# Group norm and store of an SSD chunk, issued inside the next chunk

## The chip, the cores and the metric

The kernel runs on one core of a Trainium2 chip. Five engines work from queues of their own, each in the order in which its instructions stand: PE (TensorE, matrix products; PEld is its weight load), DVE (VectorE), ACT (ScalarE), POOL (GpSimd) and SP (SyncE, which here only issues transfers). They wait for each other by semaphores. The metric is the time of one execution on the device in microseconds, the median of three.

## The reference

One step of a decoder layer over 1040 prompt rows (16 of them learned) and 32 sample rows (8 sequences of 4), with D = 1024, float32:

```
u    = rmsnorm(h);  proj = u @ w_in          # columns: conformer 2048 | z 1024 | x/B/C 1536 | dt 16
c    = silu(layernorm(dwconv31(glu(conf))))  # group A, 1024 channels
y    = ssd(silu(dwconv4(xbc)), dt)           # group B, 16 heads of 64, 2 groups, state 128, chunks of 128
y    = group_rmsnorm(y * silu(z))            # mean of squares over each group's 512 channels
h    = h + concat(c, y) @ w_out
h    = h + ffn(rmsnorm(h))                   # w_up, dwconv3, silu gate, w_down
out  = rmsnorm(h)                            # and the states of all convolutions and of the scan
```

The change concerns the line with `group_rmsnorm`. In the SSD each chunk needs the state that the chunk before it left; the norm of a chunk is needed by nothing in the scan, only by the product with `w_out`.

## The kernel before

Channels lie on partitions, rows (time) on the free axis. Products are done with each operand split into a high and a low part and three matmuls (L215 to L217, PE stage name `mm`), and the weights of a 128-column tile come by one transfer (`wr`), which ACT casts to the high part `wh` (L204) and DVE subtracts to the low part `wl` (L205).

The order of the program's middle is a list of items, `ORDER` (L59). `p` is a block of 128 conformer channels: its products, and then its convolution of width 31 on DVE, 44 multiply-adds of 128x520 in three running sums `fp` (L535), `fo` (L538) and `fs` (L541), each begun by ACT (L532, L533, L539) and joined by L544 to L547, which write the block's plane of the tile `gq`. `x` and `z` are tiles of the input projection (z tiles are evacuated by ACT at L589 and go through SiLU). `s0` and `s1` are the next SSD chunk of group 0 and 1, `q0` and `q1` the sample rows, `r0` and `r1` the sample states. `l` is a block of rows of the layer norm: it transposes all eight planes of `gq` (L862, `pt`), takes statistics on DVE (L863, L866), normalizes (`cn`, L874 on DVE, L876 on ACT) and transposes back (L883, `pb`). `h` splits the result, `c` are tiles of the product of group A with `w_out`, `y` loads and splits the normed `y` of group B.

A chunk (`ssd`, L667) loads `xc`, transposes it (L679), transposes B and forms B·C in one PSUM tile `pbt` (L696, L697), which ACT (`bt`, L698) and DVE (`cbm`, L700) evacuate. Decay matrices `ab` follow (ACT L724, L725; DVE L726), then the products `pd` (L731), `po` (L713) and the state `pst` (L751); `et` collects y on DVE (L739 to L745), is gated by z (L769) and squared by ACT (L770). The norm is L771 to L782: two sums over planes on DVE (L773, L774, `zs`), a matmul with ones that leaves the mean square of each row (L775, `pn`), DVE adds epsilon (L156), POOL raises to the power -1/2 (L157), ACT puts the result on a diagonal (L779, `rs`), a second matmul spreads it over partitions (L780, `pn` again), DVE multiplies (L781) and SP stores to `y_d` (L782). `pbt` and `pn` share a PSUM pool of two buffers (`small`), `cbm` and `zs` share a tag of two buffers; tiles of one tag are given out in the order in which the code asks for them.

No engine's queue is written by hand here. A scheduler goes through all instructions when the program is built and places, engine by engine, that ready one whose priority number is lowest. The number is the place in the code; evacuations and weight splits are raised to the front (`prio(URGENT)`), and the width-31 convolution is put behind everything else (`prio(CVP)`, CVP = 1,000,000, L523). So what is late in the code fills gaps, and the convolution fills what is left. At run time nothing is rearranged.

Of the kernel before, what the change touches and what calls it, by code (L numbers as in the profile page):

```python
# [7 lines left out]
F = mybir.dt.float32  # L8
R = mybir.dt.float32r
AF = mybir.ActivationFunctionType  # L10
ALU = mybir.AluOpType
# [3 lines left out]
P = 128  # L15
# [47 lines left out]
def hybrid_kernel(ctx: ExitStack, tc: tile.TileContext, a: dict, outs: list):  # L63
    nc = tc.nc
# [3 lines left out]
    @contextmanager  # L68
    def prio(p):
        old = tc.cur_priority  # L70
        tc.cur_priority = p
        yield
        tc.cur_priority = old
# [16 lines left out]
    y_d = dram.tile([D, T], F, name="y_d")  # L90
# [4 lines left out]
    def fmv(d):  # L95
        return d.rearrange("(k p) t -> p k t", p=P)
# [7 lines left out]
    def bank(nm):  # L104
        return ps_bk.tile([P, 512], F, tag="bk", name=nm)
# [4 lines left out]
    def small(nm):  # L110
        return ps_sm.tile([P, 512], F, tag="sm", name=nm)
# [12 lines left out]
    ident = const.tile([P, P], F, name="ident")  # L124
# [7 lines left out]
    ones = const.tile([P, P], F, name="ones")  # L132
# [3 lines left out]
    ones_g = const.tile([P, 1], F, name="ones_g")  # L136
# [17 lines left out]
    def rsqrt(dst, src, n, w=1):  # L154

        nc.vector.tensor_scalar(dst, src, EPS, None, op0=ALU.add)  # L156
        nc.gpsimd.tensor_tensor(dst, dst, mhalf[:n].to_broadcast([n, w]), op=ALU.pow)  # L157
# [68 lines left out]
    def gemm(w, kk, mh, ml, evac, chunks=(0, 1, 2), ch=CH, **kw):  # L226
        for ci in chunks:
            evac(ci, *ch[ci], products(w, kk, mh, ml, ci, ch=ch, **kw))
# [41 lines left out]
    with ExitStack() as s0:  # L270
# [28 lines left out]
        rt = [p0.tile([P, 3], F, name=f"rt{g}") for g in range(3)]  # L299
# [284 lines left out]
    def emit_z(j):  # L584
        zt = px_.tile([P, 1096], F, tag="xo", name="zo", bufs=XO)[:, 0:T]

        def ev(ci, c0, n, ps):
            with prio(URGENT):
                nc.scalar.copy(zt[:, c0:c0 + n], ps[:, :n])  # L589

        in_tile(2 * D + j * P, ev)
        nc.scalar.activation(zt, zt, AF.Silu)
        nc.sync.dma_start(z_d[j * P:(j + 1) * P, :], zt)
# [69 lines left out]
    hT = [None, None]  # L663
    sp = [None]
    left = {}

    def ssd(g, c, t0, L, mask, first=False, sample=False):  # L667
        p2 = sp[0]
        hna, xda, xdt_, xde_, rld = ((HNA0, XDA0, XDT0, XDE0, RLD0), (HNA1, XDA1, XDT1, XDE1, RLD1))[g]
        cols = slice(t0, t0 + L)  # L670
# [27 lines left out]
        nc.scalar.copy(bt[:L], pb[:L, 0:P])  # L698
        cbm = p2.tile([P, P], F, tag="cbm", name="cbm", bufs=2)
        nc.vector.tensor_tensor(cbm[:L, :L], pb[:L, P:P + L], mask[:L, :L], op=ALU.mult)  # L700
        et = p2.tile([P, 4, P], F, tag="et", name="et", bufs=2)
        if not first:
            for s in range(2):
# [45 lines left out]
        if not sample:  # L749
# [5 lines left out]
            else:  # L755
# [4 lines left out]
                else:  # L760
                    nc.vector.tensor_tensor(h8(hn), h8(hT[g]), cdt[:, c, hg:hg + 8].unsqueeze(2).to_broadcast([P, 8, 64]),
                                        op=ALU.mult)
# [3 lines left out]
        zt = p2.tile([P, 4, P], F, tag="zt", name="zt", bufs=2)  # L766
        nc.sync.dma_start(zt[:, :, :L], fmv(z_d)[:, 4 * g:4 * g + 4, cols])
        y = et[:, :, :L]
        nc.vector.tensor_tensor(y, y, zt[:, :, :L], op=ALU.mult)  # L769
        nc.scalar.activation(zt[:, :, :L], y, AF.Square)  # L770
        pn = small("pn")  # L771
        zs = p2.tile([P, P], F, tag="cbm", name="zs", bufs=2)
        nc.vector.tensor_tensor(zt[:, 0:2, :L], zt[:, 0:2, :L], zt[:, 2:4, :L], op=ALU.add)  # L773
        nc.vector.tensor_tensor(zs[:, :L], zt[:, 0, :L], zt[:, 1, :L], op=ALU.add)  # L774
        nc.tensor.matmul(pn[:L, 0:1], zs[:, :L], ones_g, start=True, stop=True)  # L775
        rt = p2.tile([P, 1], F, tag="rt", name="rt")
        rsqrt(rt[:L], pn[:L, 0:1], L)
        rs = p2.tile([P, P], F, tag="rs", name="rs", bufs=2)
        nc.scalar.activation(rs[:L, :L], ident[:L, :L], AF.Copy, scale=rt[:L])  # L779
        nc.tensor.matmul(pn[:, P:P + L], ones[:L, :], rs[:L, :L], start=True, stop=True)  # L780
        nc.vector.tensor_tensor(y, y, pn[:, P:P + L].unsqueeze(1).to_broadcast([P, 4, L]), op=ALU.mult)  # L781
        nc.sync.dma_start(fmv(y_d)[:, 4 * g:4 * g + 4, cols], y)  # L782

    def sample_h0(g, b, place):
        pool, tag = place
# [49 lines left out]
                nc.sync.dma_start(o_sssm[0, b, 8 * g:8 * g + 8].rearrange("(q two) p n -> (two p) q n", two=2), h0)  # L835

    def ssd_state_out(g):
        ph = bank("ph")
        for q in range(4):
            nc.tensor.transpose(ph[:, q * P:(q + 1) * P], hT[g][:, q * P:(q + 1) * P], ident)  # L840
        hs = sp[0].tile([P, 4, P], F, tag="zt", name="hs", bufs=2)
        nc.scalar.copy(hs.rearrange("p q n -> p (q n)"), ph)
        nc.sync.dma_start(o_pssm[0, 0, 8 * g:8 * g + 8].rearrange("(q two) p n -> (two p) q n", two=2), hs)

    def ssd_group(g):
        for c in range(8):
            yield lambda c=c: ssd(g, c, 128 * c, 128, tri, first=(c == 0))
        yield lambda: ssd(g, 8, 1024, 16, tri)
        yield lambda: ssd_state_out(g)
# [37 lines left out]
    def split_c():  # L887

        c_hi.extend(quad(f"c_hi{i}", R) for i in range(2))
        c_lo.extend(quad(f"c_lo{i}", R) for i in range(2))  # L890
        for c0, n in CHO:
            for i in range(2):
                c, hi = gq[i][:, :, c0:c0 + n], c_hi[i][:, :, c0:c0 + n]
                nc.scalar.copy(hi, c)
                nc.vector.tensor_tensor(c_lo[i][:, :, c0:c0 + n], c, hi.bitcast(F), op=ALU.subtract)
# [23 lines left out]
    def load_hr(p, m):  # L919
        c0, n = HALF[p]  # L920
        nc.sync.dma_start(H[p][:, m, 0:2 * n], ob_d[m * P:(m + 1) * P, c0:c0 + 2 * n])

    def out_c(m):
        hr = row_tile("hr")
        rows = slice(m * P, (m + 1) * P)
        nc.sync.dma_start(hr[:, F0:T], h_d[rows, F0:T])

        def ev(ci, c0, n, ps):
            with prio(URGENT):
                nc.vector.tensor_tensor(hr[:, c0:c0 + n], ps[:, :n], hr[:, c0:c0 + n], op=ALU.add)  # L930
            if ci == 2:
                nc.sync.dma_start(ob_d[rows, F0:T], hr[:, F0:T])

        return load_w(w_out[0:D, rows], KD), ev
# [40 lines left out]
    for it, item in enumerate(items):  # L975
        kind = item[0]
        if kind == "p":
            emit_pair(int(item[1:]))
        elif kind == "x":
            emit_xbc(int(item[1:]))  # L980
        elif kind == "z":
            emit_z(int(item[1:]))
        elif kind == "d":
            with tc.using_default_side("right"), tc.tile_pool(name="pdt", bufs=1) as sp[0], prio(URGENT + 3):
                emit_dt()
            with tc.using_default_side("right"):
                sp[0] = sd.enter_context(tc.tile_pool(name="ssd", bufs=1))
            work = {0: list(ssd_group(0)), 1: list(ssd_group(1))}
        elif kind == "s":
            work[int(item[1:])].pop(0)()  # L990
        elif kind == "q":
            ssd(int(item[1:]), 9, NP, NS, btri, sample=True)
        elif kind == "r":
            sample_states(int(item[1:]))
        elif kind == "l":
            if len(lblocks) == 5:
                sc.close()
                lnp = lns.enter_context(tc.tile_pool(name="pln", bufs=1))
            with prio(LNP if LNP is not None else tc.cur_priority):
                ln_part(lnp, gq, *lblocks.pop(0))  # L1000
            if not lblocks:
                lns.close()
                pfv = ctx.enter_context(tc.tile_pool(name="pfv", bufs=1))
                ffnv = pfv.tile([P, 44, 20], F, name="ffnv")
                pq = fs_.enter_context(tc.tile_pool(name="pq", bufs=1))
                ph0 = hs.enter_context(tc.tile_pool(name="ph0", bufs=6))
        elif kind == "h":
            split_c()
        elif item == "c0":

            first2 = [out_c(m) for m in range(2)]
            for ci in range(3):
                for w, ev in first2:
                    gemm(w, KD, qk(c_hi), qk(c_lo), ev, (ci,), CHO)
        elif kind == "c":
            if item == "c7":
                for m in range(KD - 1):
                    load_hr(0, m)
            w, ev = out_c(int(item[1:]))
            gemm(w, KD, qk(c_hi), qk(c_lo), ev, ch=CHO)  # L1020
        elif kind == "y":
            g = int(item[1:])
            if first_y is None:
                first_y = g
                y_quads(0, qb)
                hs.close()
                open_out()
            split_y(0, g, lambda: tmp_tile("yt"))
        if it == last_ssd:
            assert not work[0] and not work[1]  # L1030
            sd.close()
    load_hr(0, KD - 1)
    sx.close()
# [356 lines left out]
    for i in range(2, KF):  # L1390
        w = pair_weights(i)
        for p in range(2):
# [4 lines left out]
            if (i, p) == (KF - 1, 1):  # L1397
                g = g_tiles(0)
# [110 lines left out]
    for c in range(3):  # L1509
        if c == 2:  # L1510
            last_norm = LastNorm()
        hc, g = down(c, g, after)
# [32 lines left out]
```

## Time and profile before

| | |
|---|---|
| median of three runs | 1611.01 us (1605.16 to 1611.17) |
| profiled execution, its own time | 1602.27 us |
| its span, first to last instruction | 1600.6 us |
| PE busy | 1536.9 us, 96% of the span |
| DVE, ACT, POOL busy | 1164.3, 895.7, 40.4 us |
| mean granted TensorE clock | 0.980 of full speed |

The span is the time from the first to the last instruction of the profiled execution; 1.7 us lie around it. Busy PE is not PE at its peak, since the ends of matmuls are modelled; the three 358-column matmuls of a split product start some 0.16 us apart where nothing holds them. The SSD chunks lie between 334 and 732 us of the span, and the layer norm's first blocks between 534 and 565 us. The granted clock has two levels, 1.0 (2.4 GHz) and 0.5 (1.2 GHz).

### The profile page before, as it was taken

Reading aid. Unit: us, or ns where it says so; the run is one execution under the profiler, and the core shown is the slowest. Engines: PE = TensorE matmul, PEld = TensorE weight load, DVE = VectorE, ACT = ScalarE, POOL = GpSimd, SP = SyncE. Lnnn points to the kernel's source line nnn. Section 1 sums busy time; section 2 is a strip of 40 time slices with the busy share of each in tenths; the row PEclk is TensorE's granted clock in tenths of the full one; section 3 lists DMA queues with packets and bytes.
Section 4 is the critical chain, followed back from the end, with each engine's and each line's share of the span. In section 5 each row is a group of like instructions: output and inputs, shape, how many; then the busy total and the mean of one; then the engine's idle time right before and its main releaser. Section 6 shows DMA issues by size and latency. Waiting matters only on the chain.

```text
span 1600.6 us, 28038 instructions
## 1 busy us (share of the span) xinstructions
PE 1536.9 (96%) x10716; PEld 1479.4 (92%) x10716; DVE 1164.3 (73%) x1881; ACT 895.7 (56%) x2160; POOL 40.4 (3%) x99
## 2 busy tenths in 40 slices
PE   6899999999999799998999999999999999999997
PEld 5899999997999688887999999999999998999997
DVE  4799989996897758465668787777777776464343
ACT  6635545478968576684335556656655665353232
POOL 2000000000000000000000000000000000000000
PEclk9999999999999899999989999999999999999998
DMA  6321312166435329667753222222222228766553
GB/s 245 112 69 58 99 45 72 57 179 160 111 115 155 101 70 268 184 172 237 241 171 107 90 84 90 81 73 70 76 83 80 83 79 273 231 204 198 154 161 108
DMA packets 306229, 209.90 MB, mean 131 GB/s; under 512 B 28453, under 2 KB 285017, under 8 KB 306079
## 3 DMA queue, kind: packets, MB, share of 16 engines
q1 hardware_dynamic: 302654, 198.26, 41.8%
q0 software_dynamic: 1056, 5.24, 0.9%
q10 hardware_dynamic: 2384, 4.60, 0.8%
q8 instruction: 84, 1.38, 0.4%
q14 instruction: 51, 0.41, 0.1%
HBM read 157.69 MB, written 51.22 MB: 131 GB/s over the span
## 4 chain that ended last, share of the span: by engine, by line
PE 81%; DMA 6%; issue 5%; DVE 4%; ACT 2%; POOL 1%; SPq 1%; POOLq 0%; DVEq 0%; ACTq 0%
PE mm L216 11%; PE mm L215 11%; PE mm L217 11%; PE X L1249 5%; PE X L1250 5%; PE X L1251 5%; PE mmd L1429 3%; PE mmd L1427 3%; PE mmd L1428 3%; PE Z L1251 2%; PE Z L1250 2%; PE Z L1249 2%; PE Y L1250 1%; PE Y L1249 1%; PE Y L1251 1%
## 5 line engine op out<-in xcount | busy, mean ns | idle before, releaser
L204 ACT CAST wh<-wr 128x768 fp32r<-128x768 f32 (+1 forms) x130 | 131.1, 1009 | 253.6 <-PE mm L216 107.1
L215 PE MATMUL mm<-u_hi,wh 128*128 128x358 f32 (+1 forms) x816 | 268.8, 329 | 0.9 <-ACT sg L245 0.9
L217 PE MATMUL mm<-u_hi,wl 128*128 128x358 f32 (+1 forms) x816 | 268.3, 329 | 0.0
L216 PE MATMUL mm<-u_lo,wh 128*128 128x358 f32 (+1 forms) x816 | 267.6, 328 | 0.0
L205 DVE TENSOR_TENSOR wl<-wr,wh 128x768 fp32r<-128x768 f32 (+1 forms) x130 | 152.4, 1173 | 109.5 <-ACT wh L204 105.2
L1250 PE MATMUL X<-tq,wh 128*128 128x264 f32 (+1 forms) x640 | 183.4, 287 | 0.0
L1249 PE MATMUL X<-tq,wh 128*128 128x264 f32 (+1 forms) x640 | 183.0, 286 | 0.0
L1251 PE MATMUL X<-tq,wl 128*128 128x264 f32 (+1 forms) x640 | 182.7, 285 | 0.0
L1429 PE MATMUL mmd<-g,wl 128*128 128x352 f32 x528 | 171.4, 325 | 1.8 <-DVE wl L205 1.8
L1427 PE MATMUL mmd<-g,wh 128*128 128x352 f32 x528 | 171.5, 325 | 0.9 <-ACT wh L204 0.9
L1428 PE MATMUL mmd<-g,wh 128*128 128x352 f32 x528 | 169.8, 322 | 0.0
L215 PEld LDWEIGHTS mm<-u_hi,wh 128*128 128x128 f32 x816 | 153.6, 188 | 1.6 <-ACT sg L245 1.1
L217 PEld LDWEIGHTS mm<-u_hi,wl 128*128 128x128 f32 x816 | 154.0, 189 | 0.6 <-issue 0.3
L216 PEld LDWEIGHTS mm<-u_lo,wh 128*128 128x128 f32 x816 | 153.5, 188 | 0.5 <-issue 0.4
L1250 PEld LDWEIGHTS X<-tq,wh 128*128 128x128 f32 x640 | 121.7, 190 | 0.0
L1249 PEld LDWEIGHTS X<-tq,wh 128*128 128x128 f32 x640 | 120.9, 189 | 0.3 <-ACT arena L1267 0.3
L1251 PEld LDWEIGHTS X<-tq,wl 128*128 128x128 f32 x640 | 121.0, 189 | 0.0
L1342 DVE SCALAR_TENSOR_TENSOR cv<-arena,ffnv,cv 128x528 f32<-128x528 f32 (+1 forms) x88 | 67.8, 771 | 65.7 <-ACT cv L1339 65.7
L1429 PEld LDWEIGHTS mmd<-g,wl 128*128 128x128 f32 x528 | 99.3, 188 | 3.4 <-DVE wl L205 3.3
L1267 ACT COPY arena<-X 128x266 f32<-128x266 f32 (+2 forms) x200 | 63.2, 337 | 69.4 <-PE X L1251 66.7
L1427 PEld LDWEIGHTS mmd<-g,wh 128*128 128x128 f32 x528 | 99.2, 188 | 1.5 <-ACT wh L204 1.1
L1428 PEld LDWEIGHTS mmd<-g,wh 128*128 128x128 f32 x528 | 99.7, 189 | 0.0
(337 smaller groups left out, 3885.8 us busy)
## 6 DMA issues: line engine op xcount, KB each, us to landing
wr<-in_w_down_dram SPq DMA_DIRECT2D x48, 512.0 KB
wr<-in_w_in_dram SPq DMA_DIRECT2D x36, 512.0 KB
wr<-in_w_out_dram SPq DMA_DIRECT2D x24, 512.0 KB
wr<-in_w_up_dram SPq DMA_DIRECT2D x24, 512.0 KB
spare<-in_w_up_dram SPq DMA_DIRECT2D x20, 512.0 KB
wr<-in_w_down_dram SPq DMA_DIRECT2D x24, 384.0 KB
ab<-acs_d SPq DMA_DIRECT2D x32, 256.0 KB
h<-in_state_ssm_dram SPq DMA_DIRECT2D x32, 256.0 KB
```

Source lines behind the costliest of these rows:

```text
L204: nc.scalar.copy(hi[:, :kk, :], raw[:, :kk, :])
L205: nc.vector.tensor_tensor(lo[:, :kk, :], raw[:, :kk, :], hi[:, :kk, :].bitcast(F), op=ALU.subtract)
L215: mm = [nc.tensor.matmul(ps[:, :n], hi[:, k, :], xh, start=(j == 0), stop=False), nc.tensor.matmul(ps[:, :n], hi[:, k, :], xl, start=False ...
L216: nc.tensor.matmul(ps[:, :n], hi[:, k, :], xl, start=False, stop=False),
L217: nc.tensor.matmul(ps[:, :n], lo[:, k, :], xh, start=False, stop=(j == kk - 1))]
L1249: tick([nc.tensor.matmul(ps[:, :n], hi[:, k, :], bh[:, k, :], start=start and k == 0, stop=False, **kw), nc.tensor.matmul(ps[:, :n], hi[:, ...
L1250: nc.tensor.matmul(ps[:, :n], hi[:, k, :], bl[:, k, :], start=False, stop=False, **kw),
L1251: nc.tensor.matmul(ps[:, :n], lo[:, k, :], bh[:, k, :], start=False, stop=(k == 3), **kw)])
L1342: nc.vector.scalar_tensor_tensor(co[:, j0:nj], fb[:, k + j0:k + nj], ffnv[:, m, 16 + k:17 + k], co[:, j0:nj], op0=ALU.mult, op1=ALU.add)
L1427: nc.tensor.matmul(ps[:, :n], hi[:, k, :], xh, start=(k0 + k == 0), stop=False)
L1428: nc.tensor.matmul(ps[:, :n], hi[:, k, :], xl, start=False, stop=False)
L1429: nc.tensor.matmul(ps[:, :n], lo[:, k, :], xh, start=False, stop=(k0 + k == KF - 1))
```

## The change

The norm becomes a function `norm` that `ssd` puts on a list instead of running it. The next call of `ssd` (the sample rows' too) takes it off and runs it behind its own `pbt` transposes and `cbm`; `ssd_state_out`, the last item of a group, runs what is left. Nothing is computed in another way, and every engine issues the same number of instructions. What changes is each norm's place in the code, so its priority number, and the order in which `pbt`, `pn`, `cbm` and `zs` are asked for. The norm of the eighth chunk of group 0 now belongs to the first `s1`, which stands behind four z tiles, the five items `l` and `h`.

```diff
+    norms = []
...
         nc.vector.tensor_tensor(cbm[:L, :L], pb[:L, P:P + L], mask[:L, :L], op=ALU.mult)
+        if norms:
+            norms.pop(0)()
         et = p2.tile([P, 4, P], F, tag="et", name="et", bufs=2)
...
         nc.scalar.activation(zt[:, :, :L], y, AF.Square)
-        pn = small("pn")
-        zs = p2.tile([P, P], F, tag="cbm", name="zs", bufs=2)
...
-        nc.sync.dma_start(fmv(y_d)[:, 4 * g:4 * g + 4, cols], y)
+
+        def norm():
+            pn = small("pn")
+            zs = p2.tile([P, P], F, tag="cbm", name="zs", bufs=2)
+            nc.vector.tensor_tensor(zt[:, 0:2, :L], zt[:, 0:2, :L], zt[:, 2:4, :L], op=ALU.add)
+            nc.vector.tensor_tensor(zs[:, :L], zt[:, 0, :L], zt[:, 1, :L], op=ALU.add)
+            nc.tensor.matmul(pn[:L, 0:1], zs[:, :L], ones_g, start=True, stop=True)
+            rt = p2.tile([P, 1], F, tag="rt", name="rt")
+            rsqrt(rt[:L], pn[:L, 0:1], L)
+            rs = p2.tile([P, P], F, tag="rs", name="rs", bufs=2)
+            nc.scalar.activation(rs[:L, :L], ident[:L, :L], AF.Copy, scale=rt[:L])
+            nc.tensor.matmul(pn[:, P:P + L], ones[:L, :], rs[:L, :L], start=True, stop=True)
+            nc.vector.tensor_tensor(y, y, pn[:, P:P + L].unsqueeze(1).to_broadcast([P, 4, L]), op=ALU.mult)
+            nc.sync.dma_start(fmv(y_d)[:, 4 * g:4 * g + 4, cols], y)
+
+        norms.append(norm)
...
     def ssd_state_out(g):
+        while norms:
+            norms.pop(0)()
```

In the changed kernel the lines of `ssd` stand 2 to 6 lines further down (`pbt` L698 and L699, `cbm` L702, `ab` L730, `zs` L780, the two `pn` matmuls L781 and L786, the product with `pn` L787), later ones 10 lines (layer norm: `pt` L872, statistics L873 and L876, `pb` L893). All queues are word for word the same up to the first chunk's second half and again from the product with `w_out` of group B on. Between them they differ in many places; three matter below, all where the layer norm begins.

ACT, before, where it begins the convolution of the eighth and last conformer block (`fp` L532; `h0T` are states of the sample rows of `q0`, `hT` is the scan's state of group 0):

```order
L694 ACTIVATE xde<-ptx,dss 128x64 x8
L698 COPY bt<-pbt 128x128
L744 ACTIVATE xc<-xc,dbc 128x128 x3
L579 ACTIVATE xo<-xo 128x1040
L580 ACTIVATE fb<-xo 128x32
L532 ACTIVATE fp<-gq_130,confv 128x521
L533 ACTIVATE fo<-gq_130,confv 128x520
L744 ACTIVATE xc<-xc,dbc 128x32 x3
L801 COPY h0T<-ph 128x512
```

and the same start in the changed kernel:

```order
L589 COPY zo<-mm 128x358
L728 ACTIVATE ab<-ab,acs 128x128 x3
L729 ACTIVATE ab<-ab 128x512
L823 CAST rr<-kept 32x128
L532 ACTIVATE fp<-gq_130,confv 128x521
L204 CAST wh<-wr 128x1024
L589 COPY zo<-mm 128x356
L533 ACTIVATE fo<-gq_130,confv 128x520
```

The start has moved from ahead of the sample rows of `q0` to behind them and behind the next chunk of group 0 and the decays `ab` of the first chunks of group 1, into the third of the last four z tiles.

DVE, before, where that convolution ends and the layer norm's statistics (`BN_STATS`, tile `bs`) begin:

```order
L541 SCALAR_TENSOR_TENSOR fs<-fz,fsum,fs 128x520 x8
L545 TENSOR_TENSOR fs<-fs,fp 128x520
L546 TENSOR_TENSOR gq_130<-fs,fo 128x520
L863 BN_STATS bs<-pt 128x6 x3
L866 BN_AGGR mv<-bs 128x2
L205 TENSOR_TENSOR wl<-wr,wh 128x1024
L156 TENSOR_SCALAR mv<-mv 128x1
L700 TENSOR_TENSOR cbm<-pbt,tri 128x128
L868 SCALAR_TENSOR_TENSOR mv<-mv 128x1
L726 TENSOR_TENSOR ab<-ab,cbm 128x512
L874 TENSOR_SCALAR cn<-pt,mv 128x512
```

and in the changed kernel from the same `wl` on:

```order
L205 TENSOR_TENSOR wl<-wr,wh 128x1024
L702 TENSOR_TENSOR cbm<-pbt,tri 128x128
L780 TENSOR_TENSOR zs<-zt 128x128
L730 TENSOR_TENSOR ab<-ab,cbm 128x512
L156 TENSOR_SCALAR rt<-pn 128x1
...
L535 SCALAR_TENSOR_TENSOR fp<-gq_130,confv,fp 128x521
L787 TENSOR_TENSOR et<-et,pn 128x512
...
L538 SCALAR_TENSOR_TENSOR fo<-gq_130,confv,fo 128x520
...
L544 TENSOR_TENSOR gq_130<-fp,fo 128x520
...
L541 SCALAR_TENSOR_TENSOR fs<-fz,fsum,fs 128x520 x10
L545 TENSOR_TENSOR fs<-fs,fp 128x520
L546 TENSOR_TENSOR gq_130<-fs,fo 128x520
```

The last piece leaves rows out. In full, 25 of the 44 multiply-adds stand behind the `wl`, 24 of them behind the product with `pn` at L787 (3 on `fp`, 6 on `fo`, 15 on `fs`); before, all 44 stood ahead of the `wl`.

PE, before, from the last products of the z tiles to the layer norm's first transposes back:

```order
L862 MATMUL pt<-ident,gq_130 128x128 x2
L215 MATMUL mm<-u_hi_126,wh 128x356
L216 MATMUL mm<-u_lo_128,wh 128x356
L217 MATMUL mm<-u_hi_126,wl 128x356
L696 MATMUL pbt<-ident,xc 128x128
L697 MATMUL pbt<-xc 128x128
L883 MATMUL pb<-ident,cn 128x128 x14
```

and now:

```order
L217 MATMUL mm<-u_hi_126,wl 128x356
L698 MATMUL pbt<-ident,xc 128x128
L699 MATMUL pbt<-xc 128x128
L781 MATMUL pn<-ones_g,zs 128x1
L698 MATMUL pbt<-ident,xc 128x128
L699 MATMUL pbt<-xc 128x128
L786 MATMUL pn<-rs,ones 128x128
L872 MATMUL pt<-ident,gq_130 128x128 x2
L893 MATMUL pb<-ident,cn 128x128 x12
```

The two transposes of the eighth block's plane (`pt<-ident,gq_130 x2`), which need L546, stood six products ahead of the end of the z tiles; they now stand behind it, behind the norm of group 0's eighth chunk, with no product between that norm and them.

## Rows read from the trace of the kernel before

**Rows 1.** PE's waits by who was waited for, 340 to 535 us.
```profile
PE pn L775 <- DVE zs L774: 3.0, 4, 1.0
PE pn L780 <- ACT rs L779: 2.9, 7, 0.6
```
**Rows 2.** The same, 565 to 735 us (total us, times, longest).
```profile
PE pn L780 <- ACT rs L779: 4.0, 7, 2.0
```
**Rows 3.** The same, 735 to 760 us.
```profile
PE mm L215 <- ACT y_hi L910: 2.0, 3, 1.2
PE mm L216 <- DVE y_lo L911: 1.4, 3, 0.8
```
**Rows 4.** One norm in order of time: start, us, engine, line.
```profile
390.78 0.29 DVE L774 TENSOR_TENSOR zs<-zt 128x128 f32<-128x128 f32 x1
...
391.22 0.35 PE L775 MATMUL pn<-ones_g,zs 128*128 128x1 f32 x2 [1.04 <-DVE zs L774]
...
391.68 0.16 DVE L156 TENSOR_SCALAR rt<-pn 128x1 f32<-128x1 f32 x1 [0.61 <-PE pn L775]
...
392.29 0.33 PE L215 MATMUL mm<-u_hi,wh 128*128 128x356 f32 x1
...
393.01 0.49 PE L780 MATMUL pn<-rs,ones 128*128 128x128 f32 x2 [0.40 <-ACT rs L779]
...
393.26 0.41 PE L216 MATMUL mm<-u_lo,wh 128*128 128x356 f32 x1
```
**Rows 5.** PE in order of time where the layer norm begins.
```profile
534.98 0.32 PE L217 MATMUL mm<-u_hi,wl 128*128 128x356 f32 x1
535.14 0.27 PE L696 MATMUL pbt<-ident,xc 128*128 128x128 f32 x1
535.25 0.39 PE L697 MATMUL pbt<-xc 128*128 128x128 f32 x2
540.07 3.94 PE L883 MATMUL pb<-ident,cn 128*128 128x128 f32 x14 [4.44 <-DVE mv L868]
```
**Rows 6.** DVE in order of time, last block's convolution and first layer-norm block.
```profile
517.24 0.76 DVE L538 SCALAR_TENSOR_TENSOR fo<-gq,confv,fo 128x520 f32<-128x520 f32 x1
517.91 0.75 DVE L541 SCALAR_TENSOR_TENSOR fs<-fz,fsum,fs 128x520 f32<-128x520 f32 x1
...
526.04 6.31 DVE L541 SCALAR_TENSOR_TENSOR fs<-fz,fsum,fs 128x520 f32<-128x520 f32 x8
532.39 0.70 DVE L545 TENSOR_TENSOR fs<-fs,fp 128x520 f32<-128x520 f32 x1
533.12 0.70 DVE L546 TENSOR_TENSOR gq<-fs,fo 128x520 f32<-128x520 f32 x1
...
536.41 1.21 DVE L205 TENSOR_TENSOR wl<-wr,wh 128x1024 fp32r<-128x1024 f32 x1
537.53 0.15 DVE L156 TENSOR_SCALAR mv<-mv 128x1 f32<-128x1 f32 x1
...
538.52 0.68 DVE L726 TENSOR_TENSOR ab<-ab,cbm 128x512 f32<-128x512 f32 x1
539.12 0.80 DVE L874 TENSOR_SCALAR cn<-pt,mv 128x512 f32<-128x512 f32 x1
```
**Rows 7.** ACT in order of time: start of that convolution, and end of the z tiles.
```profile
472.69 0.82 ACT L532 ACTIVATE fp<-gq,confv 128x521 f32<-128x521 f32 x1 [0.62 <-DVE fs L545]
...
535.18 1.04 ACT L204 CAST wh<-wr 128x1024 fp32r<-128x1024 f32 x1 [3.61 <-PE mm L216]
...
536.48 0.27 ACT L698 COPY bt<-pbt 128x128 f32<-128x128 f32 x1
```
**Rows 8.** Busy us (x count) of PE, PEld, DVE, ACT, POOL; PEclk, DMA share, GB/s.
```profile
535.00:565.00 30.00, 20.66 (x100) 16.54 (x100) 19.06 (x41) 17.48 (x28) 3.62 (x6) 0.72 0.24 72
537.80:544.60 6.80, 4.40 (x18) 3.14 (x19) 3.08 (x8) 4.57 (x9) 1.46 (x2) 0.50 0.92 256
745.00:750.00 5.00, 4.23 (x19) 3.66 (x18) 2.24 (x4) 2.21 (x3) 0.00 (x0) 0.66 0.84 262
```

More of the change, by code (lines that the diff above doesn't have):

```diff
@@ L770, in ssd @@
         nc.scalar.activation(zt[:, :, :L], y, AF.Square)
-        pn = small("pn")
-        zs = p2.tile([P, P], F, tag="cbm", name="zs", bufs=2)
[L773 to L781, printed above, removed]
-        nc.sync.dma_start(fmv(y_d)[:, 4 * g:4 * g + 4, cols], y)
+        def norm():
[12 more added lines that the diff above has]
+        norms.append(norm)
     def sample_h0(g, b, place):
@@ L1029, in hybrid_kernel @@
         if it == last_ssd:
-            assert not work[0] and not work[1]
+            assert not work[0] and not work[1] and not norms
             sd.close()
```

## The prediction

> **What bounds the kernel now.** I read the page's table of busy time first, then PE's waits stretch by stretch, and last the order of time where a wait is long. PE bounds the kernel: nearly everything is a stream of products, and a microsecond in which PE stands is a microsecond of the total. So the reader should look for PE's waits between 334 and 760 us, since the queues are the same outside.
>
> In the scan the waits are small and of one kind. From 340 to 535 us PE waits 3.0 us for `zs` ahead of the norm's first matmul and 2.9 us for `rs` ahead of its second [rows 1]; from 565 to 735 us 4.0 us more for `rs`, 2.0 of them in one place [rows 2]. One norm in order of time shows why [rows 4]: from the first matmul at 391.22 us over DVE, POOL and ACT to the second at 393.01 us take 1.79 us, and the queue holds only two small transposes and four products between them; the last product starts at 392.29 us, so its successor could have come at about 392.45, and the norm's second matmul is some 0.5 us too early in the queue. Behind it stand products that need nothing from the norm; they start only afterwards (393.26 us). PE does not overtake.
>
> The Trainium skill says the same ("TensorE: Matmul & The Clock Gate", The mechanism): matmuls start and end in strict program order. By that rule nothing fills a gap at run time, and the rows of this norm agree; if PE could pull products forward, neither today's waits nor the hole that I forecast below would cost anything and the change would be worth about nothing.
>
> The largest single wait is elsewhere: where the layer norm begins PE has run out of products at 535.6 us and stands 4.44 us for DVE's `mv` [rows 5]. DVE had finished the last convolution at 533.82 us, its last three rows ending in L546 [rows 6], so before the change convolution and z products end together.
>
> **The change part by part.** No instruction is added or taken away, stores and loads included: 20 norms with their 20 stores move. So there are only waits to count, in three places. I count them from the profiled execution, 1602.27 us, which is 8.74 us under the median of 1611.01.
>
> *The layer norm's start.* ACT began the eighth block's convolution at 472.69 us [rows 7]. In the changed queue that start stands in the third of the last four z tiles, behind the first of its evacuations in the piece of ACT above: in products, 96 ahead of the end of the z tiles, 96 x 0.16 = 15.4 us plus some 2 us of transposes, so at about 518 us or later. And 25 of the 44 multiply-adds stand behind the `wl` that needs the weight buffer which the last z product frees. That anchor is firm: the last z product starts at 534.98 us [rows 5], ACT casts `wh` at 535.18 for 1.04 us [rows 7], so `wl` can run from 536.3 to 537.4 (1.12 us to its successor at 537.53 [rows 6]). From there on DVE, in order:
>
> - `cbm` (0.1) and `zs`, with `bt` on ACT long done (536.48 + 0.27 [rows 7]): about 537.6; from `zs` to the first norm matmul 0.44 and on to `rt` 0.46 [rows 4]: 538.5;
> - `ab`, `cbm` and one multiply-add run in the shadow of the chain over POOL and ACT, 391.68 to 393.01 = 1.33 us, then the second matmul and DVE's product with it, about 0.5 to its start and 0.6 for it, and one `ab` (0.6; each by its spacing in [rows 6]): 541.5;
> - 24 multiply-adds. Where sums alternate they start 0.67 us apart (517.24 and 517.91), where one sum runs alone 0.79 (6.35 us for 8, 526.04 to 532.39) [rows 6]. 14 x 0.67 + 10 x 0.79 = 17.3 us: 558.8;
> - L544, L547 (0.6 + 0.15, estimated as tiles of the same and of a smaller size), L545 0.73, L546 0.70 [rows 6]: 561.0.
>
> Before, the same point was 533.82. PE has only the two transposes ahead of `pb` to do once the norm is through at about 540.0: it stands from there. From L546 to `pb` took 540.07 - 533.82 = 6.25 us; of the DVE work in it `wl` (1.12), two `ab` (about 0.6 each, up to 539.12 [rows 6]) and `cbm` (0.1) are gone, 2.4 us, of which I count 2.2. `pb` at 561.0 + 4.05 = 565.1 instead of 540.07: **25.0 us later**. The cover that kept this hidden, products on PE while DVE convolves, is used up at 535.3 us, since the next products need the layer norm itself.
>
> Bounds: if ACT's start came so late that DVE is not through its first 19 multiply-adds at 536.3, it is more. 518 + about 3 us for ACT's queue + 19 x 0.67 + one `wl` (1.1) = 535; so at most 2 us more. If the DVE chain from `wl` on hides its first 4 us altogether, 21.
>
> *The waits in the norms.* Counting PE's queue between a norm's two matmuls by these spacings (0.16 a product, 0.5 a set of four small ones, 1.05 a state product), before 14 of 20 norms have 0.9 to 1.4 us of work there, against the 1.7 to 1.8 that the chain takes. In the changed queue the first matmul stands further behind `zs`, and 8 norms are short, by 0.1 to 0.45 us: 2.7 us against 8.5 before by the same count. So of the 5.9 us ahead of the layer norm [rows 1] I take 3.5 as saved (0 to 5.9: `zs` may come late again), of the 4.0 behind it [rows 2] 2.5 (0 to 4.0; a wait of ACT like that of 2.0 us may return anywhere).
>
> *The hand-over to the product of group B.* The last norm ends 38 queue rows ahead of the first product with `y_hi` before, 66 rows after: 28 x 0.16 = 4.5 us more for the last store, the load and the split. PE waited 2.0 + 1.4 us for that [rows 3], and the granted clock was 0.66 over 745 to 750 us [rows 8], 5 x 0.34 = 1.7 us. Of these 5.1 us I take 3.5 (0 to 5.1).
>
> Weight and state transfers keep their places against the products that need them; the stores that SP now issues later block nothing that PE waits for, apart from a load or two of `ab` and `xc`, which I take at nothing (0 to 2 us).
>
> **Sum:** +25.0 - 3.5 - 2.5 - 3.5 = +15.5 us. 1602.27 + 15.5 = 1617.8 in the profile's terms, and 1611.0 + 15.5 = 1626.5 against the median: I predict **1626 us**.
>
> **The rivals.**
>
> *The waits go and no hole opens* (faster). Were DVE to finish the convolution at about 534 us as before, what is left is -3.5 - 2.5 - 3.5 = -9.5, at the ends -15: 1601 us. For it speaks that the norm's waits are what the trace shows most often in the scan [rows 1, 2]; the Trainium skill's advice ("Perfetto Trace Analysis", Optimization Strategy) is to find the gaps on the engine that matters and make what they wait for start sooner, and by that advice alone one expects this. It decides at ACT's L532: it would have to run some 25 us sooner than its queue allows, and DVE's L546 stands behind PE's `pn` in any case. 4 in 100.
>
> *The hole is largely paid back* (no change). The layer norm's stage already stands or crawls: clock 0.72 over 535 to 565 us, PE busy 20.66 of 30 [rows 8]. With the chunks of group 1 further ahead in their `cbm` and `ab`, this stage and the scan behind it could give back their 9 us of standing and the waits all their 15: 25 - 17 to 25 - 24, about +4: 1615 us. Against it: the layer norm's own chain is not shortened beyond the 2.2 us counted. 10 in 100.
>
> *The hole and a colder layer norm* (slower still). PE was granted half clock from 537.8 to 544.6 [rows 8] after standing 4.44 us. After standing over 20 us the whole stage to 565 may run at that level; 0.72 against 0.50 over the 20.7 busy us is 20.7 x 0.22 / 0.5 = 9 us at most, and with none of the savings: 1611 + 25 + 5 = 1641 us. 8 in 100.
>
> **How the numbers follow.** My forecast has 78 in 100. A change within 0.5%, 8 us, is about what three runs of this kernel can't tell from none (its own spread is 6 us). The forecast's own bounds are +25.0 - 15.0 = +10 to +27; less the run spread at the low end and towards the colder stage at the high end the range is 1612 to 1639. Slower by over 0.5% (over 1619): nearly all of the forecast and all of the colder case, 0.85; same 0.11; faster 0.04.
>
> **What would show it.** PE in order of time near 540 us: one gap of 20 to 25 us ahead of the layer norm's transposes, ended by DVE's L546, with DVE busy with L535, L538 and L541 all through it. L532 on ACT near 518 to 522 us instead of 472.69. Fewer waits `pn <- rs`, together under 4 us outside the hole. `y_hi` waits under 1 us. The prediction is wrong if that gap is under 10 us (the convolution came sooner), or if the gap is there and the time is not, because the stages behind it ran shorter by more than 15 us.

## The result and the profile after

The changed kernel takes 1632.82 us in the median of four runs (1631.89 to 1636.49), the kernel before 1608.94 us beside it; the ratio is 1.016 (95% interval 1.0138 to 1.0182), so 23.9 us slower. The forecast was 1626 us in a range of 1612 to 1639. The profiled execution after took 1633.08 us (span 1631.4), near its median; that of before took 1602.27 us (span 1600.6), 6.7 us under the median of 1608.94.

PE in order of time where the layer norm begins, the answer to [rows 5] (start, us, engine, line; in brackets the wait and who ended it):

```profile
534.64 0.33 PE L217 MATMUL mm<-u_hi,wl 128*128 128x356 f32 x1
...
537.92 0.38 PE L781 MATMUL pn<-ones_g,zs 128*128 128x1 f32 x2 [2.62 <-DVE zs L780]
...
540.06 0.80 PE L786 MATMUL pn<-rs,ones 128*128 128x128 f32 x2 [1.37 <-DVE fp L535]
561.69 0.69 PE L872 MATMUL pt<-ident,gq 128*128 128x128 f32 x2 [20.83 <-DVE gq L546]
566.23 0.66 PE L893 MATMUL pb<-ident,cn 128*128 128x128 f32 x2 [3.85 <-DVE mv L878]
```

The hole stands there: the last z product starts at 534.64, where it did before (534.98), and `pb` 26.2 us later than before. Ahead of the two transposes `pt` PE stands 24.8 us in three waits; the last of them, 20.83 us, ends with L546. (The 1.37 us are put down to `fp`, but ACT's `rs` ended in the same instant, 539.61 + 0.40 us; either way it is the norm's second matmul that waits.) DVE over the same stretch, the answer to [rows 6]:

```profile
536.25 1.22 DVE L205 TENSOR_TENSOR wl<-wr,wh 128x1024 fp32r<-128x1024 f32 x1
...
537.58 0.28 DVE L780 TENSOR_TENSOR zs<-zt 128x128 f32<-128x128 f32 x1
...
540.90 0.69 DVE L787 TENSOR_TENSOR et<-et,pn 128x512 f32<-128x512 f32 x1 [0.86 <-PE pn L786]
...
552.25 7.91 DVE L541 SCALAR_TENSOR_TENSOR fs<-fz,fsum,fs 128x520 f32<-128x520 f32 x10
560.20 0.70 DVE L545 TENSOR_TENSOR fs<-fs,fp 128x520 f32<-128x520 f32 x1
560.93 0.70 DVE L546 TENSOR_TENSOR gq<-fs,fo 128x520 f32<-128x520 f32 x1
```

and ACT's start of that convolution ([rows 7]: 472.69), with the decays of group 1 ahead of it:

```profile
520.84 0.63 ACT L729 ACTIVATE ab<-ab 128x512 f32<-128x512 f32 x1
521.38 0.81 ACT L532 ACTIVATE fp<-gq,confv 128x521 f32<-128x521 f32 x1
```

DVE is never idle there for more than 0.86 us: it does the 24 multiply-adds that the late start left over. The stage in the table by stretches, busy us of PE, PEld, DVE, ACT, POOL, then the granted clock ([rows 8] had PE 20.66 busy at 0.72):

```profile
535.00:565.00 30.00, 2.56 (x12) 1.48 (x10) 28.19 (x47) 3.06 (x6) 1.36 (x2) 0.58 0.25 80
...
545.00:570.00 25.00, 4.07 (x15) 2.54 (x16) 20.93 (x36) 3.43 (x6) 1.08 (x2) 0.50 0.12 38
```

PE's waits outside the hole, for [rows 1 to 3] (total us, times, longest): first three rows 334 to 535 us, next three 565 to 735 (those of the scan), last three 735 to 790:

```profile
PE pn L786 <- ACT rs L785: 0.9, 1, 0.9
PE pn L781 <- ACT xc L748: 0.8, 1, 0.8
PE pd L735 <- DVE ab L730: 0.7, 1, 0.7
...
PE pd L735 <- DVE ab L730: 3.7, 2, 2.5
...
PE pbt L698 <- DMA xc<-x_d: 2.2, 2, 1.5
...
PE pn L786 <- ACT rs L785: 0.8, 1, 0.8
...
PE pn L786 <- ACT rs L785: 1.5, 2, 0.9
PE mm L215 <- ACT y_hi L920: 1.0, 2, 0.5
...
PE mm L216 <- DVE y_lo L921: 0.3, 1, 0.3
```

Of the norm's waits 4.0 us are left outside the hole (0.9, 0.8, 0.8 and 1.5) of 9.9, and of the hand-over's 1.3 of 3.4. In the second scan others stand in their place: `pd` for `ab` (0.4 us in the same stretch before) and `pbt` for the load of `xc` (not in the list of waits before).

### The profile page after: what moved, and what is told of

It is laid out like the page before. It is cut to its first block, busy times and chain, and to the rows that moved or that the text cites. A ratio compares the mean times of both kernels' runs of the same rounds, so it can differ in the third digit from the quotient of the medians.

```text
span 1631.4 us, 28045 instructions
## 1 busy us (share of the span) xinstructions
PE 1541.9 (95%) x10716; PEld 1481.8 (91%) x10716; DVE 1165.0 (71%) x1881; ACT 895.5 (55%) x2160; POOL 42.3 (3%) x99
## 4 chain that ended last, share of the span: by engine, by line
PE 78%; issue 7%; DMA 6%; DVE 5%; ACT 3%; POOL 1%; SPq 1%; POOLq 0%; DVEq 0%; ACTq 0%
PE mm L215 10%; PE mm L216 10%; PE mm L217 10%; PE X L1259 5%; PE X L1260 5%; PE X L1261 5%; PE mmd L1439 3%; PE mmd L1437 3%; PE mmd L1438 3%; PE Z L1261 2%; PE Z L1260 2%; PE Z L1259 2%; PE Y L1260 1%; PE Y L1259 1%; PE Y L1261 1%
```

## The experiments

The theory: ACT's late start of one convolution makes the hole, and the hole makes the time. The rivals: the norm of group 0's eighth chunk, which now stands at the layer norm's start, makes it; or it takes many deferred norms. The kernels are compared by starts on PE: the last z product, the first `pb`, the first product with `y_hi`.

**All norms deferred, the convolution begun early** (`early` is the priority of the block's own place; the same around L533 and L539):

```diff
+            with prio(early if i == 7 else CVP):
-            nc.scalar.activation(pe_, E[:, 0:HP + 1], AF.Identity, scale=wv(0), bias=wv(31))
+                nc.scalar.activation(pe_, E[:, 0:HP + 1], AF.Identity, scale=wv(0), bias=wv(31))
```

> All norms deferred as in the changed kernel; only ACT's three starts of the eighth block's convolution (L532, L533, L539 of before) take the block's own place in the code as their priority instead of 1,000,000. ACT then begins it right behind the seventh block's, and DVE's L546 and PE's last two transposes of the eighth plane stand ahead of the end of the z tiles again. Theory (the hole comes from ACT's late start): the 20.8 us wait is gone, layer norm begins near 540 us, total 24 to 26 us under the changed kernel, 1607 to 1610 us, since scan one's gain (-2.7) and the hand-over's (-6.8) about pay for what the second scan lost (+7.9). Rival (the hole comes from the norms' places on PE and DVE themselves, and the start is only one of several late things): a wait of 10 us or more stays at the layer norm, total 1618 us or more.

Measured 1609.77 us, ratio to before 1.0005 (0.9986 to 1.0023). PE at the layer norm's start:

```profile
538.38 0.33 PE L217 MATMUL mm<-u_hi,wl 128*128 128x356 f32 x1
...
542.19 0.38 PE L784 MATMUL pn<-ones_g,zs 128*128 128x1 f32 x2 [3.16 <-DVE zs L783]
...
543.01 0.41 PE L896 MATMUL pb<-ident,cn 128*128 128x128 f32 x2
544.01 0.69 PE L896 MATMUL pb<-ident,cn 128*128 128x128 f32 x2 [0.59 <-ACT cn L889]
```

The 20.8 us are gone, with every norm still deferred: the places of three instructions of ACT (the first now at 477.43 us) are worth 23.1 us, 1632.82 to 1609.77. The norm of the eighth chunk is still there, and costs 3.16 us, less than the 4.4 us that PE waited there before.

**The eighth chunk's norm direct, the others deferred.**

```diff
-        norms.append(norm)
+        if not (g == 0 and c == 7):
+            norms.append(norm)
+        else:
+            norm()
```

> Changed kernel, but the norm of group 0's eighth chunk runs directly behind its own output, as before the change; all other norms are deferred. ACT's start of the eighth block's convolution still stands where the change put it (row 490 against 489), 25 multiply-adds still behind the last z tile's wl. Theory (ACT's start): a wait of 20 to 24 us for L546 stays in one piece, the 2.6 and 1.4 us waits of that norm go, its chain no longer stands ahead of the 24 multiply-adds: 1628 to 1633 us. Rival (it is this norm, which now crosses into the layer norm's place, that makes the hole): hole gone, 1607 to 1612 us.

Measured 1632.03 us, 1.0147 (1.0113 to 1.018).

```profile
558.18 0.69 PE L875 MATMUL pt<-ident,gq 128*128 128x128 f32 x2 [24.10 <-DVE gq L546]
```

The norm that crossed into this place is not the cause: without it the hole is one wait of 24.10 us instead of three that make 24.8.

**One norm of 20 deferred** (the condition `g == 0 and c == 0` around `norms.append(norm)`, the others run at once).

> One norm of 20 is deferred, that of group 0's first chunk (at about 356 us); the other 19 run directly behind their outputs. In its order ACT begins the eighth convolution at row 491 instead of 431, behind the decays of the first s1, and 24 multiply-adds stand behind the last z tile's wl, without any norm at the layer norm's start. Theory (the hole depends on ACT's start alone, and on no norm near it): a wait of 20 to 25 us for L546, total 1628 to 1634 us. Rival (the hole needs the deferred norms): one norm out of 20 costs or gains under 2 us, 1606 to 1612 us.

Measured 1630.67 us against 1609.0, 1.0142 (1.0119 to 1.0166). ACT's start of the convolution:

```profile
521.13 0.81 ACT L532 ACTIVATE fp<-gq,confv 128x521 f32<-128x521 f32 x1
```

and PE at the layer norm's start:

```profile
535.36 0.33 PE L217 MATMUL mm<-u_hi,wl 128*128 128x356 f32 x1
...
558.92 0.69 PE L875 MATMUL pt<-ident,gq 128*128 128x128 f32 x2 [22.90 <-DVE gq L546]
```

A norm at 356 us, 180 us ahead of the hole, makes nearly all of it alone. It does so through the order: the convolution starts 60 rows later in ACT's queue. Why the scheduler no longer finds the earlier gap for it was not looked at; presumably another instruction is ready for ACT there.

**Fewer multiply-adds behind the last `wl`** (the same with `g == 0 and not sample`).

> Norms of group 0's prompt chunks deferred, those of the sample rows and of group 1 direct. PE's order at the layer norm is that of the changed kernel (the two transposes behind the eighth chunk's norm), but ACT begins the convolution at row 446 instead of 489, and 10 multiply-adds instead of 25 stand behind the last z tile's wl. Theory (the hole is DVE's work behind that wl, piece by piece): 15 pieces less at 0.67 to 0.79 us, so L546 10 to 12 us sooner than in the changed kernel, at about 550 us, a wait of 9 to 11 us instead of 20.8, total 1620 to 1624 us. Rival (PE's order alone makes the hole): the wait stays near 20 us, total 1629 us or more.

Measured 1620.93 us against 1609.0, 1.0078 (1.0056 to 1.0101).

```profile
533.87 0.33 PE L217 MATMUL mm<-u_hi,wl 128*128 128x356 f32 x1
...
537.08 0.38 PE L781 MATMUL pn<-ones_g,zs 128*128 128x1 f32 x2 [2.56 <-DVE zs L780]
539.22 0.62 PE L786 MATMUL pn<-rs,ones 128*128 128x128 f32 x2 [1.76 <-ACT rs L785]
549.52 0.69 PE L875 MATMUL pt<-ident,gq 128*128 128x128 f32 x2 [9.67 <-DVE gq L546]
```

From the last z product to `pb` it takes 20.2 us (533.87 to 554.06) instead of 31.6. These 11.4 us are 15 multiply-adds and, by DVE's rows, one `ab` (0.6) and one `cbm` (0.2) that no longer stand there, so 0.7 for each multiply-add, as expected; the median is 11.9 us less (1632.82 to 1620.93). The price follows the work behind the `wl`.

**Norms deferred in one group only** (the same with `g == 0`, and with `g == 1`).

> Norms deferred in group 0 only; those of group 1 run directly behind their outputs. Hole as in the changed kernel (+25), scan one -2.7. If the second scan's loss of some 8 us (33.5 us behind at its end after 25.6 behind at its start) is an after-effect of the hole, it is there too and the hand-over's gain is not: 1636 to 1640 us. If it comes from deferring group 1's norms, it is gone, and so is the hand-over's gain: 1629 to 1633 us.

> Norms deferred in group 1 only; group 0 as before the change, ACT's start of the eighth convolution where it was. No hole by every theory. If the second scan's loss comes from deferring group 1's norms: +7.9 there and -6.8 at the hand-over, 1608 to 1612 us. If it is an after-effect of the hole: only the gain at the hand-over is left, 1600 to 1604 us.

Measured 1633.62 us, 1.0154 (1.0125 to 1.0183), and 1606.65 us, 0.9984 (0.9966 to 1.0001). The hole belongs to group 0. On the second scan both results fall between the two expectations, which is why the kernel before was profiled again:

> The kernel before, unchanged, for a second profile. It tells how far two executions of one queue differ stage by stage. If this one is within 2 us of the first profile between the layer norm's start and the end of the second scan, the 5 to 10 us by which the changed kernel and the four variants fall behind there belong to their orders; if it falls behind by 4 us or more there too, most of that is the first profile's luck (1602.27 us, 6 us under the median of 23 runs) and no loss of the change.

One run, 1615.53 us, span 1613.8.

```profile
540.31 0.32 PE L217 MATMUL mm<-u_hi,wl 128*128 128x356 f32 x1
...
545.41 3.94 PE L883 MATMUL pb<-ident,cn 128*128 128x128 f32 x14 [4.45 <-DVE mv L868]
```

The wait at the layer norm repeats to 0.01 us, but from `pb` to the first `y_hi` this one took 4.1 us longer than the first, just past the 4 us from which the expectation puts most of what the other kernels lose there down to the first profile's luck. So one pair of profiles can't place a few us. Over the kernels, in us between the first `pbt`, those three starts and the end:

| kernel | pbt to last z | z to pb | pb to y_hi | y_hi to end |
|---|---|---|---|---|
| before, twice | 200.6, 204.2 | 5.1, 5.1 | 198.0, 202.0 | 862.5, 866.4 |
| changed | 197.1 | 31.6 | 204.4 | 860.7 |
| eighth chunk's norm direct | 197.2 | 29.6 | 203.9 | 863.2 |
| group 0 only | 198.3 | 31.0 | 203.8 | 863.9 |
| group 0's prompt chunks only | 198.3 | 20.2 | 200.3 | 862.5 |
| one norm | 200.1 | 28.1 | 200.7 | 863.7 |
| group 1 only | 200.4 | 5.1 | 201.2 | 860.9 |
| all, early start | 200.8 | 4.6 | 207.0 | 860.5 |

With the norms of group 0's prompt chunks deferred the first scan takes 197.1 to 198.3 us against 200.1 and more (but 200.8 where the convolution starts early). With group 1's deferred the second takes 201.2 to 207.0 against 198.0 to 203.8, and the rest 860.5 to 863.2 against 862.5 to 866.4: these ranges overlap, so both are tendencies and not shown.

The granted clock moves with these times too. The two profiles of before differ in the first scan by 3.6 us at a mean clock of 1.00 and 0.98, and from `pb` to `y_hi` by 4.1 us at 0.95 and 0.92. There the changed kernel had 0.95 and the one with the early start 0.91. So a part of the differences goes with the clock; but at 0.95 the changed kernel still took 6.4 us longer than the first profile of before (204.4 and 198.0).

**Does the second scan lose by a wait of SP?** The load of the decays into `et` (L704 before) waits for the landing of `y_d<-et` of two chunks earlier, since `et` has two buffers, and SP's queue stands behind it. SP's waits for that store ahead of that load, before, from 334 to 535 and from 565 to 790 us:

```profile
SPq L704 <- DMA y_d<-et: 0.6, 2, 0.4
SPq L704 <- DMA y_d<-et: 1.6, 5, 0.5
```

and in the changed kernel over the same stretches:

```profile
SPq L708 <- DMA y_d<-et: 3.5, 6, 1.3
SPq L708 <- DMA y_d<-et: 12.3, 6, 3.8
```

This wait has grown from 2.2 to 15.8 us. Is it what holds `ab` and `xc` up? First those loads were given to POOL (`nc.gpsimd.dma_start` in place of `nc.sync.dma_start`), with a control:

> As e1_starts_early (all norms deferred, no hole), but the two loads of a chunk's decays into et (L708 of the changed kernel) are issued by POOL instead of SP. With deferred norms these loads wait for the landing of the store y_d<-et of two chunks before, and SP stands for it: 6.8 us in six waits in the first scan and 10.2 in six in the second, against 0.6 and 1.6 in the kernel before; the loads of ab and xc queue behind it. Theory (this is where the gain of the deferred norms went): PE's waits pd<-ab and pbt<-xc, 1.6 and 3.1 us in e1's second scan, fall under 1.5 us together, total 1604 to 1607 us. Rival (those waits come from the order on ACT and DVE, and SP's standing is harmless): 1608 to 1612 us as e1.

> As e4_group1 (norms deferred in group 1 only, 1606.65 us), with the same two loads issued by POOL. SP's waits there were 10.7 us in six in the second scan. Theory: PE's waits pd<-ab and pbt<-xc in the second scan (2.0 and 0.7) under 1 us together, total 1602 to 1605 us. Rival: 1606 us or more.

> Control: the kernel before, with the same two loads issued by POOL. There SP stood only 0.6 and 1.6 us for these loads, so by the theory there is nothing to win: 1606 to 1611 us. If this gains 2 us or more, POOL's issue helps for another reason than the deferred store.

Measured 1631.96, 1637.19 and 1618.36 us against 1607.29: all far above what the theory gave, the control too (forecast 1606 to 1611; 1.0063, 1.0044 to 1.0083), so these three say nothing of SP. In the control POOL, 334 to 790 us, stands long for that store:

```profile
POOL et L704 <- DMA y_d<-et: 39.8, 8, 6.2
```

and PE waits for `zs` in the first scan, 3.0 us in [rows 1]:

```profile
PE pn L775 <- DVE zs L774: 8.0, 6, 3.0
```

Then the wait was taken away on SP itself:

```diff
-            nc.vector.tensor_tensor(y, y, pn[:, P:P + L].unsqueeze(1).to_broadcast([P, 4, L]), op=ALU.mult)
-            nc.sync.dma_start(fmv(y_d)[:, 4 * g:4 * g + 4, cols], y)
+            nc.vector.tensor_tensor(zt[:, :, :L], y, pn[:, P:P + L].unsqueeze(1).to_broadcast([P, 4, L]), op=ALU.mult)
+            nc.sync.dma_start(fmv(y_d)[:, 4 * g:4 * g + 4, cols], zt[:, :, :L])
```

> As e1_starts_early (all norms deferred, 1609.8 us), but the norm's product is written into zt, whose squares are used up by then, and stored from there. et is then free when DVE has read it, not when the store has landed, and its loads stay on SP. SP's waits for y_d<-et ahead of these loads (6.8 and 10.2 us in e1) are gone by construction; what is measured is what they were worth. Theory (they delayed ab and xc behind them): PE's waits pd<-ab and pbt<-xc in the second scan under 1.5 us together against 4.7 in e1, total 1602 to 1606 us, under both kernels. Rival (SP's standing is harmless, as e9 to e11 hint but don't show, since POOL's issue cost time of its own): those waits stay or others take their place, 1607 to 1612 us. In its order the two transposes of the eighth plane also stand 15 products ahead of the z tiles' end, which by e8 is worth nothing.

Measured 1609.33 us, 1.000 (0.9985 to 1.0014): the rival. SP no longer waits for the store ahead of the loads of `et`, but ahead of that of `zt`; from 565 to 790 us:

```profile
SPq L774 <- DMA y_d<-zt: 6.8, 5, 2.5
```

PE's wait for `ab` has halved there (1.6 in the kernel with the early start), that for `xc` (3.1) stays:

```profile
PE pbt L701 <- DMA xc<-x_d: 3.5, 3, 1.7
...
PE pd L738 <- DVE ab L733: 0.8, 1, 0.8
```

From `pb` to `y_hi` this kernel took 207.2 us, against 207.0 with the early start alone. The wait moved to the next buffer that the store holds. So it is shown that deferring the store makes SP wait longer, but not that this costs the second scan its time. That stays open.

**A try at a faster kernel:** norms deferred in group 1 only and the whole eighth convolution at its own priority (`prio(tc.cur_priority if i == 7 else CVP)`).

> Norms deferred in group 1 only, and the whole convolution of the eighth block at the priority of its place in the code instead of behind everything. Its end then stands 12 products ahead of the end of the z tiles, so DVE's statistics run beside some 2 us of products: of the 4.4 us wait at the layer norm 2 to 4 us go. If that and what deferring group 1 gave (1606.65 us) add up: 1602 to 1605 us. Rival: what DVE now does later (the sample rows' and the eighth chunk's y) delays the scan as much: 1606 to 1611 us.

Measured 1609.92 us, 1.0008 (0.999 to 1.0027), the rival: its L546 starts at 528.39 us, ahead of the last z product (537.12), but from that to `pb` it still took 4.6 us: DVE's part of the eighth chunk's norm, whose `zs` stood at 515.36 us before, came there instead (`zs` at 538.11). No version tried beats the kernel before beyond the measurement; group 1 alone comes nearest, its interval ending at 1.0001.

## Why the prediction held, and where it was off

**ACT's start and DVE's chain.** Forecast: L532 at 518 to 522, `wl` at 536.3, `zs` 537.6, the product with `pn` and one `ab` done at 541.5, L546 done at 561.0, `pb` at 565.1. In the trace: 521.38, 536.25, 537.58, 542.10 (start of the next), 561.63, 566.23. So the mechanism held in every step. The term of +25.0 measured 26.2 against the first profile and, counted from the last z product, 31.59 - 5.09 = 26.5. Of the 1.1 us by which `pb` came later than forecast, 0.6 lie in the norm's chain ahead of the multiply-adds: from `rt` to the second matmul 1.65 us (538.41 to 540.06) instead of 1.33, and from there to DVE's product 0.84 instead of 0.5, that matmul taking 0.80 us instead of 0.49 [rows 4] where the granted clock was 0.51 (540 to 545 us). The 24 multiply-adds took what was forecast (the last ten 7.9 us). The other 0.55 lie behind L546: from there to `pb` took 1.65 us less than before, not 2.2. PE did nothing else while it stood. The Trainium skill ("TensorE: Matmul & The Clock Gate", The mechanism) states that matmuls keep strict program order; the wait of 20.83 us agrees.

**The savings, -9.5: the term that failed.** The medians rose by 23.9 us and the hole is worth 26.5, so the savings came to some 2.6 us, not 9.5. With the hole taken away and all norms deferred the kernel is at +0.05% (-0.14 to +0.23), that is -2 to +4 us, though its first scan did not keep the gain of the changed kernel's (200.8 and 197.1 us). By terms: *the waits in the norms* ahead of the layer norm, -3.5, came out (200.6 and 204.2 us before, 197.1 after; all waits listed 5.9 us before, 2.4 after). Those behind it were forecast at -2.5, and the norm's own waits fell from 4.0 to 2.3, yet the stretch from `pb` to `y_hi` did not get shorter: 198.0 and 202.0 us before, 204.4 after, where `pd` and `pbt` wait instead. I had named a price of this kind, a load of `ab` or `xc` held up behind a late store on SP, and taken it at nothing (0 to 2 us). The waits that came are 3.7 us for `ab` and 2.2 for `xc`; that SP holds them up is not shown. *The hand-over*, -3.5: from `y_hi` to the end 862.5 and 866.4 before, 860.7 after, so 2 to 6. All stretches together make 1631.4 - 1600.6 = 30.8 us against the first profile of before and 17.6 against the second; the medians, 23.9, lie between.

Of the signs, the gap, L532 and the waits `pn <- rs` (0.9, 0.8 and 1.5 us outside the hole, under 4) came as named; the wait for `y_hi` was 1.0 us, at its limit of 1. The range was a little wider than its own working: +10 less a spread of 6 us gives 1615, not 1612.

**The rivals.** That no hole opens fell with the 20.83 us. That it is largely paid back fell too: behind `pb` the changed kernel took 204.4 + 860.7 = 1065.1 us, between the 1060.5 and 1068.4 of before, and by the medians some 2.6 us came back in all, not 17 to 24. The colder layer norm: the granted clock was at half (0.50 from 545 to 570 us), but until 561.69 PE stood there anyway. From L546 to the end of the last `pb` the mean clock was 0.88, before 0.85, and from L546 to the last `pb` it took 615.99 - 560.93 = 55.1 us, before 590.15 - 533.12 = 57.0. So the stage was not colder than before, and what half the clock would cost in it was not measured.

## What to carry to other kernels

Where a greedy scheduler fills gaps with low-priority work, any move of any instruction can change where that filler starts: read the start of the filler in the new order and count what is left of it behind the last product that covers it, before counting the waits that the change was about. Give work with a due time a priority that keeps it. And two profiles of one kernel can differ by more than the term in question (13 us here), so compare the granted clock of each stretch before reading a few us into an order, and place them by several profiles or by an experiment, not by one pair.

## What the runs showed of the hardware that I had not expected

Loads issued by POOL in place of SP cost the kernel before 11 us (1618.36 against 1607.29 us) at nearly the same time per issue (median 630 ns on POOL, 607 on SP). The rows show where, not why: the first scan took 211.3 us instead of 200.6 and 204.2, DVE waited 9.7 us for these loads instead of 4.9, and PE 8.0 us for `zs` instead of 3.0. With the norms deferred the loss lay in the second scan (`pb` to `y_hi` 222.0 and 220.4 us, in which PE waited 11.3 and 10.5 us for `zs`). POOL's queue also holds the power of every norm; which of the two delays the other was not tried.

And two executions of one queue took 200.6 and 204.2 us for the same first scan, with the norm's waits nearly equal (5.9 and 6.5 us). The granted clock was full in the first; in the second it was 0.75 and 0.91 over two pieces of 5.1 us from 356.5 us on, and 0.96 and 0.71 over two from 484.1 on. By these figures the lower clock took an estimated 5.1 x (0.25 + 0.09 + 0.04 + 0.29) = 3.4 us, nearly all of the 3.6.
